# Which engine subtracts the low parts of the MLP's weight blocks: GpSimd or VectorE

## The chip, the cores and the metric

The kernel runs on one core of a Trainium2 chip. The metric is the device time of one execution in microseconds (us); three executions of the kernel before took 2702.58, 2707.9 and 2710.39 us, so its median is 2707.9 us. Engines are called as in the profile: PE is TensorE (PEld its weight loads), DVE is VectorE, ACT is ScalarE, POOL is GpSimd, SP is SyncE, which issues most of the DMAs.

## The reference

A transformer trunk of two layers on 1024 tokens of width 1024, all in float32. Each layer has four groups of attention heads and then a squared-ReLU MLP with 4096 hidden units. The change touches the MLP alone:

```python
for l in range(DEPTH):                      # DEPTH = 2
    h = rms_norm(x, norm1_g[l])
    proj = h @ w_in[l]
    ...                                     # four attention groups -> mix
    x = x + mix @ w_out[l]
    h = rms_norm(x, norm2_g[l])
    x = x + jnp.square(jax.nn.relu(h @ w_up[l])) @ w_down[l]
return rms_norm(x, final_norm_g)
```

## The kernel before

**Three passes for one float32 product.** Both operands of a matmul are split into a high part, which is the value rounded by a copy to the type fp32r, and a low part, which is the value minus the high part. `passes` issues three matmuls for each 128x128 weight tile: high weight by high operand (line 222), high weight by low operand (L223), low weight by high operand (L224). `split` makes the parts: ACT copies to the high part (L196, or L199 with a scale) and another engine subtracts (through `tt`, L190; with a scale it is always DVE, L200). The engine of L190 is `split`'s argument `eng`: none means DVE.

**The MLP.** Weights, tokens and hidden units are cut in halves, and each product of 2x2 blocks is done as seven products of sums of blocks in place of eight products (the sums are the `raw<-raw` subtractions and additions on DVE). Its unit of work is `block`: a weight block of 128 rows x 512 columns (four 128x128 tiles, called `raw`, loaded by SP at L162), split into `wh` and `wl` by `weight_parts`, and 12 matmuls of 512 columns into one PSUM bank. Each layer has 224 blocks: 16 groups `q` of seven in `mlp_up` (`p12`, `p11`, `p6`, `p5`, `p7`, `p4`, `p3`), and 4 rounds `j` of seven times four in `mlp_down`. In `mlp_up` the operands are parts of the normed tokens (`oph`, `opl`, and the `far` tiles), in `mlp_down` they are hidden values that `mlp_up` wrote to HBM (`acts`) and that are loaded (`act`) and split again (`far<-act`).

**What follows a block.** In `mlp_up` the bank `u` is copied out by ACT after three of the seven products (L1232, L1242, L1251) before the next product adds to the same bank; DVE adds banks `p` and `q` to these copies (`ev<-p`, `ev<-q`), applies ReLU and the row scale (L1215), ACT squares (L1217), and DVE forms differences (`ev<-ev`) that are stored. The first two groups run before the norm's row scale is known; its sum of squares (`acc<-acc,sq` on DVE) goes through a matmul with ones (L265), a few tiny instructions on ACT and DVE (`rs_r`, L255) and matmuls that spread it (L299) to `rb`. In `mlp_down` DVE adds each finished bank to the residual (`x<-u,x`, `x<-p,x`).

**Buffers and order.** `wh` and `wl` have three buffers each, so the parts of a block can be made as soon as the block three before it is through. `raw` has 10 buffers, `ev` 9. Inside the MLP the order of the matmuls on PE is that in which the code is written (`manual_schedule`). On all other engines, and on PE in the attention, a list scheduler at build time sets the order of each engine's instructions by priority and by its own clock; on the chip each engine then runs its list strictly in that order, and an instruction that waits holds up all behind it.

Of the kernel before, what the change touches and what calls it, by code (L numbers as in the profile page):

```python
# [147 lines left out]
class Trunk:  # L148
# [1024 lines left out]

    def weight_parts(self, raw):
        wh, wl = (self.wp.tile([P, 4, P], R, tag="w" + p, bufs=3, name="w" + p) for p in "hl")
        self.split(wh, wl, raw, eng=self.nc.gpsimd)
        return [(wh[:, k], wl[:, k]) for k in range(4)]

    def block(self, ps, raw, ops, start=True):
# [319 lines left out]
```

## Time and profile before

| what | value |
|---|---|
| median of three executions | 2707.9 us (2702.58 to 2710.39) |
| profiled execution, its span | 2707.9 us |
| first block of the MLP on PE, layer 0 and layer 1 | 699.08 us, 2038.77 us |
| first norm of the second layer's attention on PE | 1362.13 us |
| busy PE, DVE, ACT, POOL | 2549.6, 1943.0, 1439.8, 1130.9 us |
| `wl<-raw,wh` on POOL | 448 instructions, 632.8 us |

The profiled execution's span is the median's time, and nothing lies around it. The profile gives the busy time of each engine by stretches of the span, groups of instructions with the mean of one, the waits of each engine with what ended them, and the single instructions in order of time. On DVE two instructions overlap by some 0.08 us: one that takes 0.68 us alone lets the next start after 0.60 us.

### The profile page before, as it was taken

The numbers are of one execution on the slowest core, as the hardware profiler recorded it, in microseconds if no ns is written. First come the engines' busy times: TensorE is split into PE (matmuls) and PEld (weight loads), VectorE is DVE, ScalarE is ACT, GpSimd is POOL, SyncE is SP. The second block draws the span as 40 slices with busy tenths as digits, with TensorE's granted clock in tenths as the row PEclk, the third lists the DMA queues.
The fourth block names the chain that finished last, engine by engine and source line by source line (L and its number), as shares of the span: only waits on it lengthen the run. The fifth ranks groups of instructions, "written<-read, shape, count | busy, mean of one in ns | idle before, by whom it ended". The sixth has DMA issues, their size and how long they took to land.

```text
span 2707.9 us, 37502 instructions
## 1 busy us (share of the span) xinstructions
PE 2549.6 (94%) x12296; PEld 2112.5 (78%) x12296; DVE 1943.0 (72%) x3379; ACT 1439.8 (53%) x2601; POOL 1130.9 (42%) x754
## 2 busy tenths in 40 slices
PE   8989988999899998999999999889998999999997
PEld 6778876787778887888877788668876788878886
DVE  6777866774966668887567777677749666688775
ACT  4667756664534444444436776566635344444444
POOL 2555642201345554545434656321013455544442
PEclk9989988999999999999998899899999999999998
DMA  5534597222144457444244446962221444664431
GB/s 175 169 107 129 158 287 239 82 89 63 46 144 148 153 170 267 143 142 141 95 139 134 121 113 183 295 202 69 71 71 52 154 153 152 221 221 146 136 105 63
DMA packets 186931, 389.19 MB, mean 144 GB/s; under 512 B 23712, under 2 KB 26736, under 8 KB 186736
## 3 DMA queue, kind: packets, MB, share of 16 engines
q1 hardware_dynamic: 172912, 361.62, 43.2%
q10 hardware_dynamic: 13824, 25.17, 2.7%
q8 instruction: 97, 1.59, 0.2%
q14 instruction: 98, 0.80, 0.1%
HBM read 263.29 MB, written 123.41 MB: 143 GB/s over the span
## 4 chain that ended last, share of the span: by engine, by line
PE 73%; DVE 12%; DMA 6%; ACT 4%; issue 3%; POOL 1%; SPq 0%; DVEq 0%; ACTq 0%; POOLq 0%
PE u L222 8%; PE u L224 8%; PE u L223 8%; PE mm L222 5%; PE mm L223 5%; PE mm L224 5%; PE p L222 5%; PE p L223 5%; PE p L224 5%; PE sb L810 3%; PE tr L846 3%; DVE p L812 2%; DVE part L190 2%; PE pv L835 2%; PE pv L834 2%
## 5 line engine op out<-in xcount | busy, mean ns | idle before, releaser
L190 POOL TENSOR_TENSOR wl<-raw,wh 128x512 fp32r<-128x512 f32 x448 | 632.8, 1413 | 704.8 <-ACT wh L196 691.0
L196 ACT ACTIVATE wh<-raw 128x512 fp32r<-128x512 f32 x448 | 281.5, 629 | 576.2 <-PE u L223 310.9
L190 POOL TENSOR_TENSOR wl<-ws,wh 128x512 fp32r<-128x512 f32 (+1 forms) x112 | 147.3, 1316 | 461.0 <-ACT wh L196 436.1
L222 PE MATMUL u<-far,wh 128*128 128x512 f32 x768 | 301.8, 393 | 11.4 <-ACT ev L1242 8.3
L224 PE MATMUL u<-far,wl 128*128 128x512 f32 x768 | 300.6, 391 | 2.2 <-POOL wl L190 2.2
L190 DVE TENSOR_TENSOR raw<-raw 128x512 f32<-128x512 f32 x256 | 223.1, 877 | 109.1 <-POOL wl L190 55.6
L223 PE MATMUL u<-far,wh 128*128 128x512 f32 x768 | 300.6, 391 | 0.0
L190 DVE TENSOR_TENSOR ptl<-tr,pth 128x512 fp32r<-128x512 f32 (+2 forms) x384 | 238.3, 629 | 68.5 <-ACT pth L196 66.8
L815 ACT ACTIVATE p<-p,nm 128x1024 f32<-128x1024 f32 x192 | 220.2, 1147 | 92.3 <-DVE nm L812 91.6
L196 ACT ACTIVATE pth<-tr 128x512 fp32r<-128x512 f32 (+2 forms) x384 | 205.2, 546 | 108.5 <-PE tr L846 64.9
L222 PE MATMUL p<-far,wh 128*128 128x512 f32 x640 | 252.9, 395 | 7.5 <-DVE ev L190 7.5
L224 PE MATMUL p<-far,wl 128*128 128x512 f32 x640 | 251.5, 393 | 1.5 <-POOL wl L190 1.5
L223 PE MATMUL p<-far,wh 128*128 128x512 f32 x640 | 252.2, 394 | 0.0
L810 PE MATMUL sb<-stack 96*128 96x512 f32 x640 | 217.5, 422 | 22.1 <-DVE nm L812 21.4
L190 DVE TENSOR_TENSOR far<-act,far 128x512 fp32r<-128x512 f32 x224 | 207.3, 955 | 14.7 <-ACT far L196 14.7
L190 POOL TENSOR_TENSOR p<-p 128x1024 f32<-128x1024 f32 x64 | 154.0, 2411 | 129.6 <-ACT p L898 121.3
L222 PEld LDWEIGHTS u<-far,wh 128*128 128x128 f32 x768 | 145.3, 189 | 43.5 <-ACT ev L1242 9.1
L222 PE MATMUL mm<-xh,wh 128*128 128x512 f32 x416 | 170.9, 411 | 0.8 <-DVE part L190 0.3
L224 PEld LDWEIGHTS u<-far,wl 128*128 128x128 f32 x768 | 145.2, 189 | 33.5 <-POOL wl L190 3.0
L812 DVE CUSTOM_DVE_ANT_0 p<-sb,zero,nm 128x512 f32<-128x512 f32 x192 | 142.4, 743 | 37.7 <-PE sb L810 34.6
L223 PEld LDWEIGHTS u<-far,wh 128*128 128x128 f32 x768 | 145.4, 189 | 30.0
L223 PE MATMUL mm<-xl,wh 128*128 128x512 f32 x416 | 167.7, 403 | 0.0
(245 smaller groups left out, 6110.1 us busy)
## 6 DMA issues: line engine op xcount, KB each, us to landing
act<-acts SPq DMA_DIRECT2D x224, 256.0 KB
raw<-in_w_up SPq DMA_DIRECT2D x128, 256.0 KB
acts<-ev SPq DMA_DIRECT2D x128, 256.0 KB
raw<-in_w_down SPq DMA_DIRECT2D x128, 256.0 KB
acts<-ev ACTq DMA_DIRECT2D x96, 256.0 KB
ws<-in_w_in SPq DMA_DIRECT2D x76, 256.0 KB
rz<-drows SPq DMA_DIRECT2D x40, 256.0 KB
stack<-kd SPq DMA_DIRECT2D x32, 256.0 KB
```

The lines of the kernel that those rows point to most:

```text
L190: (eng or self.nc.vector).tensor_tensor(out=out, in0=a, in1=b, op=op)
L196: nc.scalar.activation(hi, src, AF.Copy)
L222: mm(ps, w[0], x[0][:, sl], start=start, stop=False)
L223: mm(ps, w[0], x[1][:, sl], start=False, stop=False)
L224: mm(ps, w[1], x[0][:, sl], start=False, stop=stop)
L810: self.nc.tensor.matmul(ps, q[:, qt * P:(qt + 1) * P], k[:, sl], start=i == 0, stop=i == len(passes) - 1)
L812: self.nc.vector.tensor_tensor_reduce(out=p[:, sl], in0=ps, in1=self.zero[:, 0:1].bitcast(F).broadcast_to([P, 512]), scale=-scale, scalar= ...
L815: self.nc.scalar.activation(p, p, AF.Exp, bias=nm[:, 1:2], scale=-1.0, accum_out=z)
L834: nc.tensor.matmul(out, v[:, kt], h[:, sl], start=kt == 0, stop=False)
L835: nc.tensor.matmul(out, v[:, kt], lo[:, sl], start=False, stop=kt == 7)
L846: nc.tensor.transpose(t[:, k * 256 + i * P:k * 256 + (i + 1) * P], p[:, (j * 2 + k) * P:(j * 2 + k + 1) * P], self.ident)
```

## The change

The low part of each of the MLP's 448 weight blocks is subtracted on DVE and no longer on POOL. The attention's weights (`weights`, tile `ws`) stay on POOL.

```diff
     def weight_parts(self, raw):
         wh, wl = (self.wp.tile([P, 4, P], R, tag="w" + p, bufs=3, name="w" + p) for p in "hl")
-        self.split(wh, wl, raw, eng=self.nc.gpsimd)
+        self.split(wh, wl, raw)
         return [(wh[:, k], wl[:, k]) for k in range(4)]
```

The scheduler gives each subtraction a place in DVE's list, and other instructions move with it; from the second layer's attention on, the order on all engines differs, on PE too (the matmuls of the MLP keep theirs). Rows below are instructions in an engine's order, written as output<-inputs; the numbers are those of tiles.

**DVE, start of the MLP of layer 0, while PE runs the products `p11` to `p6` of the first two groups** (`v`, `t` and `far` are operands being made). Before:

```order
L190 TENSOR_TENSOR ev_7435<-q_7392,ev_7435 128x512
L190 TENSOR_TENSOR opl_7383<-t_7343,oph_7382 128x512
L190 TENSOR_TENSOR ev_7455<-q_7409,ev_7455 128x512
L190 TENSOR_TENSOR far_7618<-v_7615,far_7618 128x512
L1287 TENSOR_SCALAR v_7621<-x6_6969,par_73,v_7621 128x512
L1287 TENSOR_SCALAR t_7343<-x7_7050,par_73,t_7343 128x512
```

Now:

```order
L190 TENSOR_TENSOR wl_7546<-raw_7522,wh_7545 128x512
L190 TENSOR_TENSOR ev_7435<-q_7392,ev_7435 128x512
L190 TENSOR_TENSOR raw_7352<-raw_7352,raw_7354 128x512
L190 TENSOR_TENSOR wl_7575<-raw_7346,wh_7574 128x512
L190 TENSOR_TENSOR ev_7455<-q_7409,ev_7455 128x512
L190 TENSOR_TENSOR opl_7383<-t_7343,oph_7382 128x512
L190 TENSOR_TENSOR wl_7593<-raw_7354,wh_7592 128x512
L190 TENSOR_TENSOR far_7618<-v_7615,far_7618 128x512
L1287 TENSOR_SCALAR v_7621<-x6_6969,par_73,v_7621 128x512
L190 TENSOR_TENSOR wl_7635<-raw_7348,wh_7634 128x512
```

Between the operand pieces now stand the subtractions of the blocks that PE is about to reach. From `far_7505` to `far_7630`, the last operand of `p7`, DVE has 46 instructions in place of 36: eight `wl` and two `raw<-raw` more.

**ACT, at the same place** (`wh_7634` and `wh_7652` belong to the two `p7`, `wh_7707` to the first `p4`; `u_7434` and `u_7454` are the banks of the first two groups). Before:

```order
L196 ACTIVATE wh_7592<-raw_7354 128x512
L196 ACTIVATE far_7624<-v_7621 128x512
L1329 ACTIVATE v_7627<-x3_7155,par_73 128x512
L196 ACTIVATE wh_7634<-raw_7348 128x512
L196 ACTIVATE far_7630<-v_7627 128x512
L196 ACTIVATE far_7673<-t_7342 128x512
L196 ACTIVATE far_7676<-t_7342 128x512
L196 ACTIVATE far_7679<-t_7343 128x512
L196 ACTIVATE far_7682<-t_7343 128x512
L196 ACTIVATE wh_7652<-raw_7356 128x512
L1242 ACTIVATE ev_7573<-u_7434 128x512
```

Now:

```order
L196 ACTIVATE wh_7634<-raw_7348 128x512
L196 ACTIVATE wh_7652<-raw_7356 128x512
L196 ACTIVATE far_7624<-v_7621 128x512
L1329 ACTIVATE v_7627<-x3_7155,par_73 128x512
L1242 ACTIVATE ev_7573<-u_7434 128x512
L196 ACTIVATE wh_7707<-raw_7350 128x512
L1242 ACTIVATE ev_7591<-u_7454 128x512
L196 ACTIVATE far_7630<-v_7627 128x512
L196 ACTIVATE far_7673<-t_7342 128x512
```

The copy out of bank `u_7434`, for which PE waits before `p7`, now stands ahead of five `far` instructions that it stood behind.

**DVE, end of `mlp_up` and start of `mlp_down`, layer 0** (`far<-act` are the first operands of `mlp_down`; `ev_10031<-p_10014` reads the bank into which PE's last product `p3` is to add). Before:

```order
L190 TENSOR_TENSOR far_10133<-act_10123,far_10133 128x512
L190 TENSOR_TENSOR raw_10269<-raw_10235,raw_10237 128x512
L190 TENSOR_TENSOR far_10136<-act_10125,far_10136 128x512
L190 TENSOR_TENSOR far_10223<-act_10215,far_10223 128x512
L190 TENSOR_TENSOR raw_10235<-raw_10111,raw_10235 128x512
L190 TENSOR_TENSOR far_10226<-act_10217,far_10226 128x512
L190 TENSOR_TENSOR far_10229<-act_10219,far_10229 128x512
L190 TENSOR_TENSOR raw_10291<-raw_10239,raw_10241 128x512
L190 TENSOR_TENSOR ev_10031<-p_10014,ev_10031 128x512
```

Now:

```order
L190 TENSOR_TENSOR far_10133<-act_10123,far_10133 128x512
L190 TENSOR_TENSOR wl_10074<-raw_9889,wh_10073 128x512
L190 TENSOR_TENSOR raw_10269<-raw_10235,raw_10237 128x512
L190 TENSOR_TENSOR far_10136<-act_10125,far_10136 128x512
L190 TENSOR_TENSOR far_10223<-act_10215,far_10223 128x512
L190 TENSOR_TENSOR far_10226<-act_10217,far_10226 128x512
L190 TENSOR_TENSOR far_10229<-act_10219,far_10229 128x512
L190 TENSOR_TENSOR raw_10291<-raw_10239,raw_10241 128x512
L190 TENSOR_TENSOR raw_10235<-raw_10111,raw_10235 128x512
L190 TENSOR_TENSOR wl_10140<-raw_10111,wh_10139 128x512
L190 TENSOR_TENSOR ev_10031<-p_10014,ev_10031 128x512
```

Two `wl` come in ahead of that read. From the first `far<-act` of `mlp_down` to the first `x<-p` DVE has 57 instructions in place of 49, the eight more being `wl`.

## The prediction

> **What bounds the kernel now.** I read the page's busy times first, then the busy times by stretch, PE's waits in the MLP, and last single instructions in order of time. A row of the stretches gives the stretch, its length, then busy us and instructions of PE, PEld, DVE, ACT and POOL, PE's granted clock, the DMA share and GB/s.
>
> ```profile
> span 2707.9 us, 37502 instructions
> PE 2549.6 (94%) x12296; PEld 2112.5 (78%) x12296; DVE 1943.0 (72%) x3379; ACT 1439.8 (53%) x2601; POOL 1130.9 (42%) x754
> ```
>
> ```profile
> 691.00:1357.00 666.00, 645.84 (x2808) 530.13 (x2807) 487.73 (x592) 300.73 (x505) 321.14 (x227) 0.98 0.44 146
> 698.86:727.20 28.34, 23.73 (x98) 17.65 (x96) 27.60 (x38) 15.05 (x27) 9.48 (x6) 1.00 0.13 38
> 1024.00:1063.80 39.80, 32.79 (x135) 25.96 (x134) 39.24 (x49) 20.18 (x37) 19.39 (x12) 0.96 0.69 244
> 812.00:1016.00 204.00, 204.00 (x896) 168.00 (x895) 133.24 (x160) 84.70 (x149) 106.71 (x75) 1.00 0.48 158
> 1083.00:1354.00 271.00, 271.00 (x1197) 224.56 (x1196) 197.10 (x237) 122.30 (x194) 132.46 (x98) 1.00 0.41 130
> 2035.00:2700.00 665.00, 636.26 (x2770) 522.53 (x2768) 491.33 (x609) 301.46 (x522) 315.13 (x223) 0.98 0.42 140
> ```
>
> The long middle parts of the MLP (812 to 1016, 1083 to 1354) are PE alone: busy 204.00 of 204.00 and 271.00 of 271.00 us, 204/896 = 0.228 us a matmul and 2.73 us a block of 12. Nothing that DVE or POOL does there moves the end as long as the parts of a block come in time. PE is idle for 666.00 - 645.84 = 20.2 us in one layer's MLP and 28.7 in the other's, all of it at the ends of the stages. There DVE is the full engine: 27.60 of 28.34 us at the start of `mlp_up`, 39.24 of 39.80 at the start of `mlp_down`. PE's waits there, of layer 0, and the last row of the tail:
>
> ```profile
> PE u L222 <- ACT ev L1242: 4.1, 1, 4.1
> PE mm L299 <- DVE rs_r L255: 2.5, 1, 2.5
> PE u L222 <- ACT ev L1232: 3.8, 1, 3.8
> PE p L222 <- DVE ev L190: 3.8, 1, 3.8
> PE u L224 <- POOL wl L190: 2.2, 1, 2.2
> PE u L299 <- DVE rs_r L255: 3.9, 2, 2.6
> ```
>
> **The price of one subtraction, and its refund.** Next the instruction itself, on POOL, and the DVE form that it becomes (same shapes and types, `far`); the three figures are minimum, median and maximum in ns. Then DVE and POOL side by side, and DVE's means in 1083 to 1354 for an instruction with both inputs in SBUF and for one with an input in PSUM.
>
> ```profile
> L190 POOL TENSOR_TENSOR wl<-raw,wh x448: 1277/1297/4237, 691.7 to 2682.6; 128x512 fp32r<-128x512 f32 x150
> L190 DVE TENSOR_TENSOR far<-act,far x224: 672/680/1784, 1024.0 to 2644.5; 128x512 fp32r<-128x512 f32 x112
> ```
>
> ```profile
> 705.00 0.68 DVE L190 TENSOR_TENSOR raw<-raw 128x512 f32<-128x512 f32 x1
> 705.60 0.68 DVE L190 TENSOR_TENSOR opl<-t,oph 128x512 fp32r<-128x512 f32 x1
> ...
> 708.07 1.76 DVE L1287 SCALAR_TENSOR_TENSOR t<-x,par,t 128x512 f32<-128x512 f32 x1
> 709.75 1.77 DVE L190 TENSOR_TENSOR far<-t,far 128x512 fp32r<-128x512 f32 x1
> ```
>
> ```profile
> 707.71 3.27 POOL L190 TENSOR_TENSOR wl<-raw,wh 128x512 fp32r<-128x512 f32 x2 [9.32 <-ACT wh L196]
> ```
>
> ```profile
> L190 DVE TENSOR_TENSOR far<-act,far 128x512 fp32r<-128x512 f32 x84 | 79.2, 971 | 7.3 <-ACT far L196 7.3
> L190 DVE TENSOR_TENSOR x<-u,x 128x512 f32<-128x512 f32 x53 | 36.2, 684 | 45.0 <-PE u L224 45.0
> ```
>
> On DVE a `wl` costs 0.60 us of queue (705.00 to 705.60). But DVE pays already: while POOL runs its two, from 707.71 on, two DVE instructions take 1.76 and 1.77 us in place of some 0.7; and only instructions with two SBUF inputs are stretched (971 ns against 684). So a `wl` on POOL costs DVE up to 1.09 us, and that is refunded. In 1024 to 1063.8 the 49 DVE instructions would take 29.4 us at 0.60; they are busy for 39.24: 9.8 us of stretch for 12 POOL instructions, 0.82 each. At the start of `mlp_up`, 36 instructions (38 with the cut ones) at about 0.62 would be 22.3 to 23.6 of the 27.60: 4 to 5.3 us for 6. So where DVE is full, the move about pays for itself.
>
> **Term 1, middle of the stages: 0.** In 812 to 1016 DVE goes from 133.24 us to at most 133.24 + 75 x 0.60 = 178 of 204, in 1083 to 1354 to 197.10 + 98 x 0.60 = 256 of 271, without any refund; PE stays full. In the new list a `wl` stands two blocks ahead of its use (behind the addition of block b comes the `wl` of b+3), which is 5.4 us; 0.6 for ACT's copy and 0.7 for itself leave about 4.1 us of slack. Bounds: 0 to the loss of the burst rival below.
>
> **Term 2, start of `mlp_up`: 2.5 us less in each layer.**
>
> ```profile
> 729.38 0.79 PE L222 MATMUL u<-far,wh 128*128 128x512 f32 x1 [4.14 <-ACT ev L1242]
> 729.97 0.63 PE L223 MATMUL u<-far,wh 128*128 128x512 f32 x1
> ...
> 739.92 1.84 PE L265 MATMUL mm<-ones,acc 128*128 128x1 f32 x16
> ```
>
> ```profile
> 745.85 1.25 DVE L255 SCALAR_TENSOR_TENSOR rs_r<-rs_t,rs_r 128x8 f32<-128x8 f32 x1
> 755.47 0.69 DVE L190 TENSOR_TENSOR raw<-raw 128x512 f32<-128x512 f32 x1 [1.18 <-POOL wl L190]
> 759.58 7.18 DVE L190 TENSOR_TENSOR ev<-ev 128x512 f32<-128x512 f32 x8
> ```
>
> PE's 4.14 us wait is for ACT's copy L1242, which stood behind five `far` copies and now stands ahead of them. It was followed by matmuls of 0.63 us (0.43 from start to start) until 733.8, some 10 x 0.2 = 2 us more. That wait goes. What is late next is the norm's sum: L265 at 739.92 needs DVE's last `acc`, and DVE's list up to `far_7630` now holds 46 x 0.62 = 28.5 us of work in the 28.34 it had. So L265 comes at about 739.4, 0.5 sooner, after a new idle of some 6 us on PE; the second `p4` behind it may then run at the slower rate (12 x 0.2 = 2.4 us). The Trainium skill's "TensorE: Matmul & The Clock Gate" (Why this matters for your kernels) has PE drop to half rate after gaps above about 3 us, and by it the 2.4 us are sure and L299 gains only 0.5 us. Behind L265, `rs_r` loses its 1.25 us stretch and two `raw<-raw` that ran before it, so L299 comes 0.5 to 2 us earlier. Up to the copy L1232 that ends the 3.8 us wait, DVE loses the 1.18 us wait for POOL and about 1.1 us at each of three stretched instructions (eight `ev<-ev` take 7.18, not 4.9), and gains four `wl` of 0.60: 1 to 1.5 us. Together 2 to 3.5; I take 2.5. Bounds for a layer: 0, if L265 is not earlier and the rest breaks even, and 6.1, the whole first wait with its slow matmuls.
>
> **Term 3, start of `mlp_down`: 1.5 us less in each layer.**
>
> ```profile
> 1019.99 4.09 DVE L190 TENSOR_TENSOR ev<-ev 128x512 f32<-128x512 f32 x4 [0.70 <-ACT ev L1217]
> ...
> 1033.28 0.68 DVE L190 TENSOR_TENSOR ev<-p,ev 128x512 f32<-128x512 f32 x1
> ...
> 1063.83 0.68 DVE L190 TENSOR_TENSOR x<-p,x 128x512 f32<-128x512 f32 x1
> ```
>
> PE's 3.8 us wait is for the `ev<-p` at 1033.28, the fifteenth DVE instruction from 1019.99 on. Now the first of these `ev<-ev` starts an estimated 1.2 us later (a `wl` ahead of it waits for ACT's copy), and 17 instructions of 0.60 stand before `ev<-p`: 1021.2 + 10.3 = 1031.5, so `p3` starts 1.8 us sooner, with some slow matmuls less. After it PE needs a `wl` each 2.73 us from a list that is full: the one of the fourth block stands at about 1046.8 and is done at 1047.5, where POOL's let PE go on at 1049.45 (the 2.2 us wait); one more block waits about 0.9. That leaves 1.1 us, or 2 with the slow matmuls spared. DVE itself reaches the `x<-p` of 1063.83 with 57 x 0.60 in place of 39.8 us, some 5 us sooner, but PE doesn't wait for that. Bounds: 2 us more, if two blocks more wait, to 4 less.
>
> **Term 4, tail: 1 us less.** DVE's last sums run after POOL's last `wl` at 2682.6; the `rs_r` wait before it (one of the 3.9 us) ends some 0.6 us earlier by stretch saved, and the adds of the last blocks about as much. Bounds: 1 more to 2 less.
>
> **Term 5, the second layer's attention: 0, plus or minus 5 us.** Its instructions are the same, in another order of the scheduler. The two layers are the one row on what another order is worth:
>
> ```profile
> 27.50 1.68 PE mm L265 x16
> 1362.13 1.68 PE mm L265 x16
> ```
>
> ```profile
> 699.08 0.39 PE L222 MATMUL q<-oph,wh 128*128 128x512 f32 x1
> 2038.77 0.39 PE L222 MATMUL q<-oph,wh 128*128 128x512 f32 x1
> ```
>
> From the norm's L265 to the MLP's first block it takes 671.6 us in layer 0 and 676.6 in layer 1: 5.0 us between two orders of the same work. I see no reason for a sign.
>
> **Sum.** 2 x 2.5 + 2 x 1.5 + 1 = 9 us less than the profiled execution's 2707.9 us, which is also the median of the runs: 2699 us. More than the idle of 20.2 + 28.7 us and its slow matmuls can't be won.
>
> **Rivals.**
>
> *No change that can be told* (I take 0.3%, 8 us, as what a measurement of this kernel can tell from none). The starts of the stages are bound by DVE, and its work there comes out even: if terms 2 and 3 end at 0 to 1, the time is 2704 to 2708. For it speaks that 46 x 0.62 equals the 28.34 us before; against it that PE's two longest waits hang on the order of ACT and DVE, which changes for the better.
>
> *Slower: bursts of DVE work in `mlp_down`.* Once in each round `j` DVE has its 16 `raw<-raw` in a row; the new list has 53 instructions in 12 blocks, 53 x 0.60 = 31.8 us against 12 x 2.73 = 32.8. Before, DVE was as full there, but the `wl` were in another queue. At more than 32.8 + 4.1 (the slack) over 53 = 0.70 us an instruction PE begins to wait; at 0.75 it would lose 53 x 0.75 - 36.9 = 2.9 us in each of six bursts (three rounds, two layers): 2708 - 9 + 17 = 2716. For it speaks that a `wl` now waits for ACT with all of DVE behind it; against it that DVE's row of 0.60 leaves 1 us of room even without the slack.
>
> *Slower: no refund.* If DVE's stretch isn't POOL's doing, each `wl` in a DVE-bound stretch costs 0.60: 8 + 4 at the start of `mlp_up`, 8 at that of `mlp_down`, 20 x 0.60 x 2 layers = 24 us: 2732. Against this rival stand 0.68 with POOL idle and 1.76 with POOL at work. The Trainium skill's "Perfetto Trace Analysis" (Optimizing Scalar/DVE Operations) would rather move work off a saturated DVE, even to GpSimd, and so speaks against this change; it adds that the two share a read port, so that such a move might not help, and there the trace agrees (971 ns against 684).
>
> *The attention's order turns out worse* by 5 us or more, which takes half of the gain or all of it: 2704 and up.
>
> **How the numbers follow.** The forecast, 2690 to 2703 us: 0.54. No change to tell, 2704 to 2710: 0.17. Bursts or another wait behind a `wl` in DVE's list: 0.14. No refund: 0.05. A worse order of the attention: 0.10. Of the forecast's case 0.10 ends within 8 us of the time before, and of the attention's 0.05. So faster by over 0.3% is 0.44, within 0.10 + 0.17 + 0.05 = 0.32, slower 0.14 + 0.05 + 0.05 = 0.24. The range goes from 2684 (terms 2 and 3 at 4 us, attention 3 less) to 2720 (bursts, or a bad order with one more wait).
>
> **What would show it.** `wl` on DVE at 0.68 us, POOL at 1130.9 - 632.8 = 498 us, DVE between 1943 us (every `wl` refunded in full) and 1943 + 448 x 0.68 = 2248 (none), at some 2050 if the refund is 0.45 us each, between the 0.82 of the full stretch and (133.24 - 160 x 0.68)/75 = 0.33 of the middle of `mlp_up`, with `far<-act` back at 0.68; no 4.1 us wait for L1242, a wait before L265 in its place; PE still full in the middle parts. Wrong it would be if PE shows waits for DVE's `wl` in every round or group, if `far<-act` stays near 0.97, or if the second attention takes more than 680 us.

## The result, and the profile after

The changed kernel takes 2698.85 us (median of 19 executions, 2692.41 to 2704.7), the kernel before on the same chip 2706.69 us (19, 2700.89 to 2712.96). The ratio is 0.9970, with a 95% interval of 0.9961 to 0.9978: 7.8 us faster, just about the 0.3% that can be told from no change. Predicted were 2699 us.

The profiled execution of the changed kernel is the fastest of the 19: 2692.41 us, of which the span is 2690.6. So the totals below are compared by the runs' medians, and of the profiles only single stages. (The time around the span, which the text above put at nothing, is 1.8 us there, and 1.7 to 3.5 us in the other executions.)

The page of the kernel after, its span and busy times, and the groups of DVE that are to be held against those of before:

```profile
span 2690.6 us, 36835 instructions
PE 2545.8 (95%) x12296; PEld 2107.6 (78%) x12296; DVE 2014.2 (75%) x3827; ACT 1442.9 (54%) x2601; POOL 496.9 (18%) x306
```

```profile
L190 DVE TENSOR_TENSOR wl<-raw,wh 128x512 fp32r<-128x512 f32 x448 | 306.8, 685 | 76.9 <-ACT wh L196 75.6 <-PE u L223 1.3
...
L190 DVE TENSOR_TENSOR raw<-raw 128x512 f32<-128x512 f32 x256 | 174.6, 686 | 6.7 <-DMA raw<-in_w_up 2.0 <-DVE t L1287 0.3
L190 DVE TENSOR_TENSOR far<-act,far 128x512 fp32r<-128x512 f32 x224 | 150.7, 684 | 1.8
```

DVE has 448 instructions more and is busy for only 71 us more: these groups, all with two SBUF inputs, are back at 0.68 to 0.69 us, now that POOL does next to nothing in the MLP. The group `raw<-raw` took 877 ns each before:

```profile
L190 DVE TENSOR_TENSOR raw<-raw 128x512 f32<-128x512 f32 x256 | 223.1, 877 | 109.1 <-POOL wl L190 55.6 <-DMA raw<-in_w_up 51.6
```

The busy times by stretch of the kernel after (columns as above): the start of `mlp_up` and that of `mlp_down`, where DVE is the full engine, then the long middles of the two.

```profile
695.24:723.58 28.34, 25.62 (x108) 19.66 (x106) 27.64 (x46) 16.76 (x30) 0.00 (x0) 1.00 0.16 47
1020.40:1060.20 39.80, 34.45 (x141) 27.44 (x142) 39.80 (x67) 18.70 (x33) 0.00 (x0) 0.96 0.74 256
808.40:1012.40 204.00, 204.00 (x896) 167.88 (x895) 151.14 (x230) 86.10 (x150) 0.00 (x0) 1.00 0.49 159
1079.40:1350.40 271.00, 271.00 (x1198) 224.46 (x1197) 214.67 (x329) 123.04 (x192) 4.81 (x3) 1.00 0.41 128
```

In the same 28.34 us DVE gets through 46 instructions where it was 38, in the same 39.80 us through 67 where it was 49. PE is full in the middles, 204.00 of 204.00 and 271.00 of 271.00 us, as before. PE's waits after, first at the start of `mlp_up` in layer 0, then at the start of `mlp_down`, last in the tail:

```profile
PE mm L265 <- DVE acc L190: 4.5, 1, 4.5
PE u L222 <- ACT ev L1232: 4.1, 1, 4.1
PE p L224 <- DVE wl L190: 1.5, 2, 0.8
PE u L224 <- DVE wl L190: 1.1, 1, 1.1
PE u L223 <- DVE far L190: 0.6, 1, 0.6
```

```profile
PE u L224 <- DVE wl L190: 3.0, 1, 3.0
PE p L222 <- DVE ev L190: 1.3, 1, 1.3
PE u L222 <- ACT ev L1251: 1.0, 1, 1.0
PE u L222 <- ACT ev L1242: 0.6, 1, 0.6
```

```profile
PE u L299 <- DVE rs_r L255: 3.5, 2, 2.3
PE u L265 <- DVE ev L190: 2.2, 1, 2.2
```

The 4.1 us wait for L1242 and the 2.5 us wait for `rs_r` are gone from the first list. In their place PE waits 4.5 us for DVE's last `acc`, ahead of L265, and for `wl` and `far` 3.2 us, where it waited 2.3 us for POOL's `wl`.

**Where the time went.** A layer's MLP is measured from its first block on PE to the next norm's L265, or to the end of the span. Before, then after:

```profile
699.08:1361.97 662.89, 642.73 (x2794) 527.56 (x2792) 485.95 (x588) 297.94 (x500) 319.25 (x226) 0.98 0.45 147
2038.77:2707.90 669.13, 632.49 (x2753) 519.42 (x2751) 492.92 (x612) 298.83 (x517) 312.53 (x221) 0.97 0.43 142
```

```profile
695.47:1354.66 659.19, 641.19 (x2793) 526.42 (x2792) 522.34 (x808) 299.21 (x500) 6.80 (x5) 0.99 0.46 147
2026.02:2690.60 664.58, 632.08 (x2753) 518.56 (x2751) 524.17 (x832) 300.20 (x517) 0.00 (x0) 0.98 0.44 143
```

The two MLPs are shorter by 3.7 and 4.55 us, 8.2 together, which is the measured 7.8 as nearly as it can be. The profiles differ by 17 us; the other 9 lie in the two attentions, and the second experiment shows that differences of this size there are those of one execution to another.

### The profile page after: what moved, and what is told of

Its sections match the earlier page's. It is cut to its first block, busy times and chain, and to the rows that moved or that the text cites. A ratio compares the mean times of both kernels' runs of the same rounds, so it can differ in the third digit from the quotient of the medians.

```text
span 2690.6 us, 36835 instructions
## 1 busy us (share of the span) xinstructions
PE 2545.8 (95%) x12296; PEld 2107.6 (78%) x12296; DVE 2014.2 (75%) x3827; ACT 1442.9 (54%) x2601; POOL 496.9 (18%) x306
## 4 chain that ended last, share of the span: by engine, by line
PE 74%; DVE 12%; DMA 6%; ACT 4%; issue 3%; POOL 1%; SPq 0%; DVEq 0%; ACTq 0%; POOLq 0%
PE u L222 8%; PE u L224 8%; PE u L223 8%; PE mm L222 5%; PE mm L223 5%; PE mm L224 5%; PE p L222 5%; PE p L223 5%; PE p L224 5%; PE sb L810 3%; PE tr L846 2%; DVE p L812 2%; DVE part L190 2%; PE pv L835 2%; PE pv L834 2%
## 5 line engine op out<-in xcount | busy, mean ns | idle before, releaser
L190 DVE TENSOR_TENSOR wl<-raw,wh 128x512 fp32r<-128x512 f32 x448 | 306.8, 685 | 76.9 <-ACT wh L196 75.6
L190 POOL TENSOR_TENSOR wl<-ws,wh 128x512 fp32r<-128x512 f32 (+1 forms) x112 | 146.5, 1310 | 1107.0 <-DMA saved<-x 664.1
L190 DVE TENSOR_TENSOR raw<-raw 128x512 f32<-128x512 f32 x256 | 174.6, 686 | 6.7 <-DMA raw<-in_w_up 2.0
L224 PE MATMUL mm<-xh,wl 128*128 128x512 f32 x416 | 166.5, 400 | 0.0
```

The lines of the kernel that those rows point to most:

```text
L190: (eng or self.nc.vector).tensor_tensor(out=out, in0=a, in1=b, op=op)
L224: mm(ps, w[1], x[0][:, sl], start=False, stop=stop)
```

## The experiments

Stage times in this part are read from each run's profile by the same marks: first block `q<-oph` of a layer, start of the last matmul into a bank `q` (eight blocks before the end of `mlp_up`, so that the wait of its last `p3` counts to "down"), next norm's L265 or the end of the span. "up" and "down" are the two parts of an MLP so split. Each kernel's time is set against that of the kernel before, run beside it on the same chip. "Rest" is the difference of the medians less the difference of the two MLPs. It stands for all that the MLPs don't explain, and holds the second attention. By the intervals of the ratios (about 3 us either way) and the spread of a stage it is good to some 4 us.

| kernel | ratio and 95% interval | us against before | MLP 0 (up, down) | MLP 1 (up, down) | second attention | rest |
|---|---|---|---|---|---|---|
| before | | | 662.9 (310.2, 352.7) | 669.1 (310.1, 359.0) | 676.8 | |
| after | 0.9970 [0.9961, 0.9978] | -7.8 | 659.2 (307.0, 352.2) | 664.6 (306.8, 357.8) | 671.4 | +0.4 |
| up alone | 1.0024 [1.0014, 1.0034] | +6.3 | 660.1 (307.3, 352.8) | 667.7 (307.6, 360.1) | 688.8 | +10.5 |
| down alone | 0.9971 [0.9959, 0.9983] | -7.8 | 663.0 (310.1, 352.9) | 667.3 (309.6, 357.7) | 672.6 | -6.1 |
| starts alone | 0.9989 [0.9979, 0.9999] | -3.7 | 659.1 (306.7, 352.4) | 664.3 (305.2, 359.1) | 675.1 | +4.9 |
| middles alone | 0.9977 [0.9968, 0.9986] | -6.2 | 663.0 (310.0, 353.0) | 667.7 (310.2, 357.6) | 674.7 | -4.9 |
| layer 1 alone | 0.9985 [0.9975, 0.9996] | -4.1 | 662.8 (308.8, 354.0) | 665.2 (307.2, 357.9) | 669.1 | -0.1 |
| layer 0 alone | 0.9986 [0.9975, 0.9996] | -3.7 | 659.7 (306.1, 353.6) | 668.2 (309.0, 359.2) | 675.6 | +0.4 |
| POOL subtracts too | 1.0774 [1.0756, 1.0791] | +209.5 | 764.5 (373.4, 391.1) | 771.5 (368.4, 403.1) | 673.0 | +5.5 |
| POOL copies | 1.0022 [1.0012, 1.0032] | +5.1 | 665.2 (310.4, 354.8) | 672.3 (311.0, 361.3) | 672.6 | -0.4 |
| POOL writes zeros | 0.9967 [0.9957, 0.9977] | -6.3 | 660.1 (307.9, 352.3) | 663.5 (306.0, 357.5) | 677.3 | +2.1 |
| no low parts | 0.9855 [0.9836, 0.9873] | -37.4 | 641.9 (296.8, 345.1) | 645.1 (297.0, 348.1) | 685.1 | +7.6 |
| mixed version | 0.9954 [0.9941, 0.9967] | -10.9 | 660.5 (309.0, 351.5) | 664.1 (305.4, 358.8) | 671.1 | -3.5 |

**1. Which part of the MLP: four kernels.** `mlp_up` alone and `mlp_down` alone on VectorE:

```diff
         with tc.manual_schedule(engines={mybir.EngineType.PE}), \
...
+            self.low = None
             self.mlp_up(l, acts)
+            self.low = self.nc.gpsimd
             self.mlp_down(l, acts)
...
+        self.split(wh, wl, raw, eng=self.low)
```

> The low parts are subtracted on VectorE in mlp_up alone; mlp_down keeps GpSimd. Theory of the stage starts: the start of mlp_up gains what it gained in the whole change (PE's first q block to the end of the two first groups, about 2 us a layer), mlp_down keeps its old waits of 3.8 and 2.2 us: about 4 us less than before, 2703. Rival, the gain lies in the other order of the second layer's attention: the MLP stages are as long as before, and the time follows that order alone, 2702 to 2712. Rival, the gain lies in the middle of mlp_down: 2707.

The other way round, with `gpsimd` ahead of `mlp_up` and `None` ahead of `mlp_down`:

> The low parts are subtracted on VectorE in mlp_down alone; mlp_up keeps GpSimd. Theory of the stage starts: the start of mlp_down and the tail gain about 2 us a layer, the start of mlp_up keeps its 4.1 us wait for L1242: about 4 us less than before, 2703. Rival, the attention's order: the MLP stages as long as before, 2702 to 2712. Rival, no refund at a full VectorE: 2712 and more.

Then the starts of the stages alone (first three groups and the last group of `mlp_up`, first round of `mlp_down`), and all but these. The first line shown is in `mlp_up`'s loop, which begins at the third group, the second in `mlp_down`'s; ahead of `mlp_up` stands `self.low = None` for the first two groups.

```diff
+                self.low = None if q in (2, 15) else self.nc.gpsimd
...
+                self.low = None if j == 0 else self.nc.gpsimd
```

> VectorE subtracts for the first three and the last group of mlp_up and for the first round of mlp_down, GpSimd for the rest. Theory of the stage starts: nearly the whole gain, 2699 to 2701, since PE is full elsewhere with either engine; the tail keeps GpSimd. Rival, the middle counts: half of the gain or less, 2703 and more.

> The opposite of the one before: GpSimd for the first three and the last group of mlp_up and the first round of mlp_down, VectorE for the rest. Theory of the stage starts: no gain but the 1 us of the tail, 2706, with PE full in the middle. Rival, the middle counts: 2699 to 2703. Rival, the attention's order: any time from 2702 to 2712, with the MLP stages as before.

Measured: `mlp_up` alone is slower by 6.3 us, `mlp_down` alone faster by 7.8, the starts alone faster by 3.7, the middles alone by 6.2. All four totals miss what the theory expected, and the last two fall where the rival "the middle counts" put them. By the totals the parts don't add up. By the stages they do. Leaving aside the kernels in which GpSimd works beside VectorE or no low parts are made, every "up" with VectorE at its start takes 305.2 to 307.6 us and every "up" with GpSimd there 308.8 to 310.2, whatever the other parts do; the middles alone leave it at 310.0 and 310.2. From the 251st to the 1251st matmul of a layer, the middle of `mlp_up`, it takes 228.3 us, and from the 1701st to the 2601st, `mlp_down` behind its first round, 204.0 us, in every kernel of the table but the one in which POOL subtracts too. So the middles cost nothing on either engine. Behind them, the tail of layer 1 takes 41.7 to 41.9 us with VectorE there and 42.1 to 43.2 with GpSimd, 0.6 us on the mean. What lies between "up" and the 1701st matmul, the start of `mlp_down`, is shorter with VectorE by 0.6 us in layer 0 and 0.7 in layer 1 on the mean, while kernels of the same kind differ by up to 2.2 us there. So the gain lies at the start of `mlp_up`, with a little in the tail; what the start of `mlp_down` adds is less than its scatter.

What spoils the totals is the rest: +10.5 for `mlp_up` alone, some -5 or -6 for `mlp_down` alone and for the middles alone, +4.9 for the starts alone; those near 5 are hardly over its error. The second attention comes in another order on PE in each of these four kernels. In `mlp_up` alone PE's list of waits in it holds two that stand out. In the kernel before the first isn't there, and the second is 0.3 us:

```profile
PE sb L982 <- DVE nb L1058: 5.2, 2, 4.2
PE mm L265 <- DVE sq L190: 4.2, 1, 4.2
```

Its second attention takes 688.8 us, of which PE is busy 632.67; before it was 676.80 and 629.12. The two waits are 9.1 us longer; others in the list are shorter (8.0 us for `pth` at L1003 went to 2.3), and PE's idle time in all is 8.5 us more. So the two are not the whole account of the 12.0, and why the scheduler's order brings them was not looked into.

**2. One layer at a time.** If the second attention's order is what disturbs, a kernel that changes layer 1's MLP alone must be free of it: PE's whole list is that of the kernel before, instruction by instruction, and so are the other engines' up to the MLP of layer 1. The kernel with layer 0 alone has `l == 0` in the same line.

```diff
+            self.low = None if l == 1 else self.nc.gpsimd
```

> VectorE subtracts the low parts in the second layer's MLP alone. The scheduler's lists up to the end of the second attention are those of the kernel before, so only the last stage differs. Theory (the gain is in the starts of the MLP's stages, 4.5 us in layer 1 by the profile after: 669.1 to 664.6 us): the second attention stays near 677 us as before, the last MLP takes 664 to 665 us, the time is 2703 us (ratio 0.998). Rival (the gain came from the second attention's new order): the last MLP is shorter too, but the total must then be no faster than 2706. A ratio under 0.9975 would say that layer 1's MLP gains more than the profile shows.

> VectorE subtracts the low parts in the first layer's MLP alone. The MLP of layer 0 should take 659 us in place of 662.9 (3.7 us less), that of layer 1 669 us as before. The second attention comes in some order of the scheduler's. Theory: its order is a lottery that the change draws a ticket in; the profiles so far span 671 to 689 us for it, so the total is 2704 plus whatever this stage differs from 677 us. Rival (the attention is the same work and costs the same whatever the order): it takes 675 to 679 us and the total is 2703 to 2705.

Both came as expected: 4.1 us for layer 1 and 3.7 for layer 0, which add up to the whole change's 7.8. In both the rest is zero within its error.

One thing in these profiles did not come as expected. The second attention of the kernel before, and the same lists in the kernel with layer 1 alone:

```profile
1361.97:2038.77 676.80, 629.12 (x3342) 526.37 (x3340) 469.77 (x1076) 412.50 (x781) 246.32 (x150) 0.96 0.48 140
```

```profile
1362.08:2031.13 669.05, 627.21 (x3342) 523.26 (x3340) 469.02 (x1080) 413.31 (x781) 242.29 (x147) 0.96 0.48 142
```

The same work in the same order takes 7.75 us less in one execution than in another. So a single profile says little of an attention's order, and the 5.4 us that the second attention is shorter in the profile after are within that. What an order is worth can be read from the medians, through the rest. The kernels that share an order of PE with the kernel after (layer 0 alone, POOL copies, POOL writes zeros) have rests of +0.4, -0.4 and +2.1, after itself +0.4. (The one in which POOL subtracts too has this order as well; its +5.5 is the remainder of 209 and tells nothing.)

**3. What stretches VectorE: three kernels.** The changed kernel, and beside it an instruction on GpSimd for each block, into a spare tile: the same subtraction again, a copy of the high part, or zeros.

```diff
         self.split(wh, wl, raw)
+        spare = self.wp.tile([P, 4, P], F, tag="ws", bufs=2, name="spare")
+        self.tt(spare, raw, wh.bitcast(F), ALU.subtract, self.nc.gpsimd)
```

with the last line in the second and the third kernel as

```diff
+        self.nc.gpsimd.tensor_copy(spare, wh.bitcast(F))
```

```diff
+        self.nc.gpsimd.memset(spare, 0.0)
```

> The kernel after, and GpSimd makes the same 448 subtractions once more into a spare tile that nobody reads. Theory (GpSimd's work beside VectorE's stretches instructions with two SBUF inputs, and the change pays since this goes): far<-act in the middle of mlp_down returns from 0.68 us to 0.9 to 1.0, VectorE's busy time rises by 120 to 250 us over after's 2014, and the time is 2711 to 2740 us. Rival (no refund, the stretch isn't GpSimd's doing): far<-act stays at 0.68 and the time stays at 2699.

> The kernel after, and GpSimd copies each high part into a spare tile: it reads one operand from SBUF and not two, and is tied to the blocks' pace by that. Theory (any reading from SBUF by GpSimd stretches VectorE's instructions with two SBUF inputs): far<-act at 0.75 us or more, VectorE's busy time well over 2014 us, and the time over 2705, up to the 2917 of the second subtraction. Rival (only GpSimd's instructions with two SBUF inputs do it): far<-act at 0.68 to 0.70, the time 2697 to 2701.

> The kernel after, and GpSimd fills a spare tile of the same size with zeros for each block, so that it is busy but reads nothing. Theory (the stretch comes from GpSimd's reading from SBUF beside VectorE): no stretch, far<-act at 0.68 to 0.70 us, the time 2697 to 2703. Rival (any GpSimd work on SBUF stretches VectorE, its writes too): far<-act at 0.75 or more and the time 2705 or more.

The subtraction: the stretch is back, as the theory had it. DVE in the middle of `mlp_up`, by groups, and that stretch as a whole:

```profile
L190 DVE TENSOR_TENSOR wl<-raw,wh 128x512 fp32r<-128x512 f32 x66 | 64.6, 979 | 5.4 <-ACT wh L196 5.4
L190 DVE TENSOR_TENSOR raw<-raw 128x512 f32<-128x512 f32 x38 | 43.9, 1154 | 10.4 <-DMA raw<-in_w_up 8.8
```

```profile
820.00:1040.00 220.00, 188.45 (x782) 144.86 (x780) 197.27 (x205) 74.77 (x130) 108.43 (x65) 0.99 0.37 121
```

The time was missed by far: 2917 us, where 2711 to 2740 were expected. The expectation counted the stretch and forgot that the price stays beside it. At 197.27 / 205 = 0.96 us an instruction, the 230 instructions that DVE has in 204 us of PE in the kernel after would take 221 us, and DVE's own waits, 22.7 of these 220 us, come on top: DVE's list is now slower than PE in the middle too, and `mlp_up` goes from 307 to 373 us. The prediction's burst rival put the threshold at 0.70 us an instruction; here it is passed. GpSimd's own subtraction is held up too: its median is 1692 ns, against 1297 for the `wl` before.

The zeros: these waited for no data, so the scheduler let 222 of each layer's 224 run in one go at the start of the MLP, and in the later parts there were none. POOL is busy for 104 us on end, across the stretch in which DVE is full (first its row, then DVE's from 700 to 800 us):

```profile
677.58 104.02 POOL L1178 MEMSET spare<- 128x512 f32 x222
```

```profile
L190 DVE TENSOR_TENSOR wl<-raw,wh 128x512 fp32r<-128x512 f32 x27 | 18.5, 686 | 13.0 <-ACT wh L196 13.0
```

With POOL at full work beside it up to 781.6 us, DVE's groups stand where they stand in the kernel after, at 682 to 688 ns, and the slower ones of L200 and L1287 (L1289 here, as the added lines shift it) at 743 to 750, where they take 742 to 748 after, and the gain against before is 6.3 us, where it is 7.8 after. So GpSimd's writing costs DVE nothing that shows.

The copies read one operand. They stretch too, though less (DVE in the middle of `mlp_down`, then POOL's copies there):

```profile
L190 DVE TENSOR_TENSOR wl<-raw,wh 128x512 fp32r<-128x512 f32 x96 | 84.4, 879 | 0.1
L190 DVE TENSOR_TENSOR far<-act,far 128x512 fp32r<-128x512 f32 x84 | 63.1, 765 | 0.0
L190 DVE TENSOR_TENSOR x<-u,x 128x512 f32<-128x512 f32 x55 | 37.6, 684 | 25.1 <-PE u L224 25.1
```

```profile
L1178 POOL COPY spare<-wh 128x512 f32<-128x512 f32 x96 | 65.2, 679 | 196.0 <-ACT wh L196 196.0
```

DVE is busy for 2117.4 us in all, 103 more than after: 0.23 us a copy, where the second subtraction costs (2356.5 - 2014.2) / 448 = 0.76 each. Against the kernel before it is 5.1 us slower, where the kernel with the zeros is 6.3 faster. "Up" takes 310.4 and 311.0 us, as long as before, though in layer 0 PE no longer waits for the copy L1242 there; it waits 5.3 us for `acc` and 4.1 for `wl`. With the zeros it takes 307.9 and 306.0. So the new order of ACT and DVE alone doesn't bring the gain at the start of `mlp_up`: where much of the refund is missing, the gain is gone.

So it is GpSimd's reading from SBUF that holds up DVE's instructions with two SBUF inputs, and how long depends on how long it reads; those with an input in PSUM take 679 to 690 ns on the mean, by group, in all of these kernels. The traces show how. In the kernels with the subtractions and with the copies, of the five commonest forms with two SBUF inputs that ran beside one such GpSimd instruction, those that started over 0.1 us ahead of it (237 and 163) took 0.67 to 0.70 us, so none was stretched, and GpSimd's ended 1.2 us (a subtraction) or 0.5 us (a copy) behind them on the median. Those that started behind it ended 0.56 us behind its end at the latest. So whichever starts first holds up the other. The longest of each, DVE starting 0.02 us behind POOL (two rows of the kernel with the subtractions, two of that with the copies):

```profile
1163.90 1.30 POOL L190 TENSOR_TENSOR spare<-raw,wh 128x512 f32<-128x512 f32 x1 [1.43 <-ACT wh L196]
1163.92 1.82 DVE L190 TENSOR_TENSOR wl<-raw,wh 128x512 fp32r<-128x512 f32 x1
...
957.70 0.62 POOL L1178 COPY spare<-wh 128x512 f32<-128x512 f32 x1 [1.89 <-ACT wh L196]
957.72 1.14 DVE L190 TENSOR_TENSOR wl<-raw,wh 128x512 fp32r<-128x512 f32 x1
```

The stretch is 1.82 - 0.68 = 1.14 us beside a subtraction of 1.30 and 1.14 - 0.68 = 0.46 beside a copy of 0.62: in both, GpSimd's instruction but for 0.16 us. The Trainium skill's "SBUF — State Buffer" (Who interferes with whom) states that a DVE instruction with two SBUF inputs contends with a GpSimd instruction that reads SBUF, and not with one that only writes it. All three runs agree with that. Its stronger statement (SBUF: two separate sides), that the one that starts first takes the shared ports for its whole instruction and the other fully blocks, fits these rows but for the 0.16 us.

**4. The refund without the price.** No low parts are made, by either engine; the third matmul of a pass takes the high part in place of the low one.

```diff
-        wh, wl = (self.wp.tile([P, 4, P], R, tag="w" + p, bufs=3, name="w" + p) for p in "hl")
-        self.split(wh, wl, raw)
-        return [(wh[:, k], wl[:, k]) for k in range(4)]
+        wh = self.wp.tile([P, 4, P], R, tag="wh", bufs=3, name="wh")
+        self.nc.scalar.activation(wh, raw, AF.Copy)
+        return [(wh[:, k], wh[:, k]) for k in range(4)]
```

> The low parts of the MLP's weights are not made at all: no subtraction on either engine, and the third matmul of each pass takes the high part again (so the low part's share is left out of the product, and the time alone counts). This shows the refund without the price. Theory: VectorE is busy for after's 2014 less its 448 subtractions of 306.8, so 1707 us, 236 less than before: the refund is 0.53 us a subtraction. Each MLP stage gets shorter than after's 659.2 and 664.6 by part of the price in the full stretches (20 subtractions of 0.60 a layer, 12 us, of which perhaps 4 to 8 on the path): 653 to 657 and 657 to 661 us, the time 2684 to 2693. Rival (the starts are not bound by VectorE, and the gain came from the order of ACT's copies): the MLP stays at 658 to 660 and 663 to 665, the time at 2697 to 2700.

The time is 2672 us, where 2684 to 2693 were expected. The MLPs take 641.9 and 645.1 us, 17.3 and 19.5 less than after, three times what was expected. The row of layer 0's MLP, and all its waits of PE at the start of `mlp_up`:

```profile
699.06:1340.99 641.93, 635.69 (x2794) 523.63 (x2792) 394.48 (x588) 304.28 (x499) 6.53 (x4) 0.99 0.46 151
```

```profile
PE u L222 <- ACT ev L1232: 2.9, 1, 2.9
PE u L222 <- ACT ev L1242: 2.0, 1, 2.0
```

PE's idle time is 6.2 us, where it is 18.0 after and 20.2 before. PE's busy time is another 5.5 us less (635.69 for 641.19), most of it, some 4 us by the spacing of the matmuls, because fewer run slowly behind a wait. The estimate had only DVE's own 0.60 us for 20 subtractions, part of it hidden; what goes besides are PE's waits for a `wl` itself (5.6 us in the two lists of after) and the slow matmuls behind each wait. DVE is busy for 1757.2 us, 50 more than expected, since one subtraction adds less to DVE's busy time than its own 0.685 us, instructions in a row overlapping: 257 us of price for 448, 0.57 each, and 186 of refund, the difference being the 71 us above.

Seen from before, then, taking the subtractions off both engines is worth 21 us in layer 0's MLP, and putting them on DVE costs 17.3 of these again. The change trades one cost for another nearly as large. The attention's order is another one here, and a bad one by the rest (+7.6).

**5. A mixed version.** GpSimd keeps `mlp_up` of layer 0, VectorE has all else; the order of the second attention is then that of `mlp_down` alone, whose rest was -6.

```diff
+            self.low = self.nc.gpsimd if l == 0 else None
             self.mlp_up(l, acts)
+            self.low = None
             self.mlp_down(l, acts)
```

> In layer 0 GpSimd subtracts in mlp_up and VectorE in mlp_down (the lists up to the end of the second attention are those of the run with VectorE in mlp_down alone); in layer 1 VectorE subtracts everywhere. Theory (stages add up, and that run's 2699.85 us, with only 1.7 us gained in its MLPs, hides a second attention that costs 6 us less in this order): the last MLP falls by another 3 us, to 664.5, and the time is 2697 us, a little below after's 2699. Rival (the second attention's order is worth nothing, and that run was fast for another reason): 2700 to 2704.

It takes 2698.33 us, and the kernel before, run beside it, 2709.23: 0.9954 [0.9941, 0.9967]. Its MLPs give 7.4 us of the 10.9, and the rest is -3.5, for the same order that gave -6.1: together they speak for some 5 us that come from the order alone. Against the kernel after (0.9961 to 0.9978) the intervals overlap, so that it is the faster of the two isn't shown.

## Why the prediction was right, and where it wasn't

- **The price and its refund: right.** A `wl` takes 685 ns on DVE, `far<-act` is back at 684, POOL is busy for 496.9 us (498 predicted) and DVE for 2014 (some 2050 predicted). The refund is 186 / 448 = 0.42 us a subtraction, where 0.45 was taken; the estimate of 2050 had 0.68 us for the price, the instruction's length, where it is 257 / 448 = 0.57, and that makes up the difference. That GpSimd's reading is the cause, the third experiment shows.
- **Term 1, the middles, 0: right.** PE is at 204.00 of 204.00 and 271.00 of 271.00, and by the first experiment the middles take the same time with either engine.
- **Term 2, start of `mlp_up`, -2.5 a layer: right in its walk, a little small.** Measured 3.2 and 3.3 in the profile after, and 3.1 as the mean over nine stages of each kind in the runs. From the first block on, L265 of the second group comes after 40.1 us, where it was 40.8 (0.5 sooner was predicted, without its working, and 0.7 it is). The new wait before it is 4.5 us, where some 6 were put; beside it stand the short waits for `wl` and `far`, 3.2 us in all against 2.3 before. The next rows are PE's:

```profile
735.59 1.87 PE L265 MATMUL mm<-ones,acc 128*128 128x1 f32 x8 [4.54 <-DVE acc L190]
...
737.89 0.63 PE L223 MATMUL u<-far,wh 128*128 128x512 f32 x1
...
742.58 2.39 PE L299 MATMUL mm<-ident,rs_r 128*128 128x128 f32 x16
...
760.00 0.50 PE L222 MATMUL u<-oph,wh 128*128 128x512 f32 x1 [4.11 <-ACT ev L1232]
...
760.57 0.60 PE L224 MATMUL u<-oph,wl 128*128 128x512 f32 x1
...
763.52 0.61 PE L222 MATMUL u<-oph,wh 128*128 128x512 f32 x1
```

  All twelve matmuls of the second `p4` run at the slower rate, and L299 stands 47.1 us behind the first block where it was 48.1: 1.0 sooner. The case in which the slow matmuls are sure, and L299 gains 0.5, was nearer than the 2 us at the other end. From there to the block behind the copy L1232, DVE's shorter list gives another 1.0 (1 to 1.5 in the term): that block starts 64.5 us after the first one, where it was 66.5. What is left to 3.2 wasn't in the term. Behind this wait eight matmuls are slow (760.57 to 763.52), and before there were fourteen, all at 0.60 us or more:

```profile
765.56 0.79 PE L222 MATMUL u<-oph,wh 128*128 128x512 f32 x1 [3.85 <-ACT ev L1232]
...
771.27 0.61 PE L223 MATMUL p<-far,wh 128*128 128x512 f32 x1
```

  Six slow matmuls fewer at 0.2 us are the missing 1.2. How many there are behind a wait differs from one profile to the next: behind the 4.1 us wait for L1242, with GpSimd in `mlp_up` of layer 0, it was 7, 8, 11, 12 and 13 in five of them. So this part is no property of the change.
- **Term 3, start of `mlp_down`, -1.5 a layer: right in its walk, too large.** The two waits named are there: `p3` waits 1.3 us in place of 3.8, and the `wl` of the fourth block 3.0 in place of 2.2. Leaving out what `mlp_up` had gained, `p3` starts 1.6 us sooner (1.8 predicted), and PE goes on behind that `wl` 1.95 us sooner, as the term had it. But the start of `mlp_down` is only 0.5 us shorter in layer 0 and 0.7 in layer 1, and on the mean of the runs 0.6 and 0.7, no more than its scatter. The term took the slow matmuls behind `p3`'s wait as partly spared; they come behind the 3.0 us wait instead:

```profile
1040.68 0.79 PE L224 MATMUL u<-far,wl 128*128 128x512 f32 x1 [3.00 <-DVE wl L190]
```

- **Term 4, tail, -1: right in sign, too large.** The waits for `rs_r` and for `ev` before the end are 3.5 and 2.2 us, where they were 3.9 and 3.2. The tail is 0.5 us shorter, 0.6 on the mean of the runs; matmuls at the slower rate behind the waits take back the rest.
- **Term 5, the second attention, 0 give or take 5: right for this change, with a bound that was too narrow and was taken from a poor row.** The rest of after is +0.4. But orders of other kernels gave +10.5 and about -5, and two layers of one profile can't bound it: the same order alone moves by 7.75 us between executions.
- **The rivals.** No refund fell (experiment 3). The bursts don't show in the kernel after, where DVE's 329 instructions take 214.67 of 271 us and PE is full; DVE holds PE up in the middle as soon as its instructions are stretched to 0.96 us. A worse order of the attention did not come here and did come in the kernel with `mlp_up` alone, which is slower than before by its rest. "No change that can be told" is the near miss: 7.8 us are just short of the 8 that were named, and only the interval of the ratio, 0.9961 to 0.9978, tells them from none.

The sum, with the means over the runs' stages: 2 x 3.1 + 0.6 + 0.7 + 0.6 = 8.1 us, where 9 were predicted and 7.8 measured. That the time came out within 0.2 us of the forecast is luck: term 2 was 1.2 us too small for its two layers and terms 3 and 4 together 2.1 too large, and the 2707.9 us from which the 9 were taken are 1.2 above the median of the 19 executions.

## What to carry to other kernels

An instruction moved from GpSimd to a full VectorE is not all price: as long as GpSimd reads SBUF, a VectorE instruction with two SBUF inputs that starts behind it waits for it, and that is refunded; weigh the two in the stretches where VectorE is full, since elsewhere neither counts. A net of 8 us can be the difference of a cost of 21 to 24 us and one of 17 to 20 in each layer, so the next step is to get rid of the work there and not to move it. Where a list scheduler orders all engines, a small edit can move the total by 5 to 10 us in a stage that it doesn't touch: compare stage by stage, and keep a variant whose lists up to that stage are unchanged.

## What was not expected of the hardware

PE's granted clock falls after shorter waits than the gaps of about 3 us that the prediction cited. In the kernel without low parts, a wait of 2.01 us is enough (the matmuls, then a row of stretches from the slow ones on):

```profile
723.17 0.50 PE L222 MATMUL u<-far,wh 128*128 128x512 f32 x1 [2.01 <-ACT ev L1242]
...
723.85 0.63 PE L224 MATMUL u<-far,wh 128*128 128x512 f32 x1
...
726.41 0.63 PE L224 MATMUL u<-far,wh 128*128 128x512 f32 x1
```

```profile
723.58:726.99 3.41, 3.41 (x10) 2.63 (x9) 2.69 (x5) 3.41 (x8) 0.00 (x0) 0.50 0.44 100
```

In the kernel before, the wait of 2.19 us for POOL's `wl` is followed by a stretch at full clock:

```profile
1049.45:1052.86 3.41, 3.41 (x15) 2.80 (x16) 3.41 (x3) 2.74 (x5) 3.14 (x3) 1.00 0.61 222
```

The slow matmuls begin 0.7 us behind the wait of 2.01 and last some 3 us; after 4.11 us of idle (760.00 above) they begin 0.6 us behind it, after 4.54 at once. So not the length of the wait alone decides. The clock stands at 0.50 for 3.41 us here, for 3.42 behind the wait for L1232 in the kernel after (from 760.58) and for 6.83 behind that wait in the kernel before (from 764.91), which is why eight matmuls are slow in the one and fourteen in the other. The Trainium skill's "TensorE: Matmul & The Clock Gate" (What's actually happening) has a free-running window of about 3.4 us in which the activity is watched, and these lengths, one window or two, fit it; its advice, no gaps above about 3 us (Why this matters for your kernels), is too generous here. By these rows the wait of 2.0 us costs PE 3.4, with seven matmuls at 0.2 us more.
